# Half-precision filters with both orders prepared together, and spaced sums of the first layer's gate and up weights with the context's pass in half precision

## The chip, the cores and the metric

The kernel runs on one core of one Trainium2 chip. The metric is the device time of one execution, in microseconds (us). The core has TensorE (PE, with its weight loads as PEld), VectorE (DVE), ScalarE (ACT), GpSimd (POOL) and SyncE (SP); each takes its instructions in order, and SP, ACT and POOL also issue transfers (DMA), each on a queue of its own.

## What is computed

Two layers of a backbone over 1024 latent tokens and 256 context tokens, with 1024 channels. The first layer mixes half of its channels with a Fourier transform and half with two orders of a long convolution (Hyena); its filters are made by a small network and normalised. The second layer is a neighbourhood attention. Each layer ends with a gated feed-forward part. Cut to what the change touches:

```
h = sin(freq * (z @ w1 + b1)); h = sin(freq * (h @ w2 + b2))
h = (h @ w3).reshape(L, 2, HY_ORDER, HY_CH)
h = h * exp(-t01 * deltas)
h = h / sum(abs(h), axis=(0, 1))
v = x1 * long_conv(v, filt[:, 0], skip[0])       # order 0
v = x2 * long_conv(v, filt[:, 1], skip[1])       # order 1
u = modulate(rms_norm(x, g), shift, scale)       # shift, scale from silu(c) @ ada_w + ada_b
y = (silu(u @ w_gate) * (u @ w_up)) @ w_down     # latent and, in layer 0, context tokens
```

All inputs are float32.

## The kernel before, in words

Precision is kept by splitting an operand into a high and a low part and adding three products (high x high, high x low, low x high). Many stages do this in float16 with a scale per weight ("half precision" below, `half_split`, L1218 and L1219: ACT writes the high part, DVE the low part); others use the 4-byte format fp32r (`split`, L287 and L289). A float16 split of weights needs a scale, taken from a bound on the weights: `abs_sums` (L1251) lets ACT add up the absolute values of a tile, and `scale_cols` turns the sums into a scale.

The program is written as generators that yield between pieces of work; the caller decides by its `next` calls how the pieces interleave. That order, the buffers of each pool and a planner that orders the instructions of each engine by modelled durations set the order of the work. `issue_after` (and `follow`) asks the planner to issue something only after a given instruction. The pools that matter: "s4" (20 tiles of 128x1024 f32), "s2" (34 of 128x512 f32), the weight tags "ws", "wh" and "wl" (two tiles each), and PSUM with eight banks, six called "ps" and two "pq".

The stages up to the Winograd products of the first layer:

- `filter_mlp` (L566) makes the hidden features for 512 latent and 128 context positions. `filter_raw` (L612) multiplies them with w3 and the decay window: for each order it adds and subtracts two blocks of w3 (L626), splits them, and runs 32 matmuls of 512 columns for the latent tokens, which DVE evicts (L646).
- `filter_spectrum` (L684) turns the raw filters of an order into their spectrum: 4 families x 4 blocks x 4 frequency blocks x 3 matmuls. For each block DVE forms an operand (L706 to L713), `split` makes two fp32r parts, and `cmat` (L321) loads a float16 matrix into a "ws" tile and lets ACT convert it to fp32r in a "wh" or "wl" tile (L335). ACT evicts the results (L750). `filter_sum` (L650) interleaves the normalising sum: absolute values on ACT, a maximum (L660) and an addition (L662) on DVE.
- `ada_first` (L408) multiplies the conditioning with the first 2048 columns of the adaLN weights, which POOL's queue loads into "wh" and "wl" tiles (`mat`), and turns the result (L431 to L441). `norms` (L2140) squares the rows of the tokens (L2149), spreads the norms by small matmuls, and normalises the tokens block by block (L555 to L558). In `run` (from L2196) the adaLN product comes before the spectrum of order 0, during the filters of order 0; the filters of order 1 are woven into the spectrum of order 0.
- `in_proj` (L779) runs 16 column blocks of the input projection; the steps of the context's filters and spectra (`filt`) and of four adaLN groups (`ada`) are its fill.
- `out_proj` (L1178) runs two groups of eight column blocks; its fill is `qkv_sums` (L1253), which loads 44 weight tiles over POOL's queue and sums them on ACT: four for layer 0's first gate and up tiles, 32 for the second layer's projections, eight for layer 1. `first_scales` makes scales of them. `after1` (in `run`) normalises the context with fp32r parts.
- `ffn` for layer 0 first runs the context pass: 22 blocks x gate and up x 24 matmuls of 256 columns, weights split into fp32r by `weights`; each block's result goes through a SiLU (L1529) and a product (L1530). Then come the latent tokens by Winograd products in half precision (`wino_weights`, `wino_steps`, L1449). Where a weight tile has no scale yet, `wino_weights` takes its sums itself, on ACT, before the split.

## Time and profile before

| | |
|---|---|
| timed runs | median 2919.48 us of 3 (2914.33 to 2921.39) |
| profiled execution | 2919.95 us, span 2918.2 us |
| mean granted TensorE clock | 0.977 |
| PE busy | 2766.6 us (95% of the span) |
| DVE, ACT, POOL busy | 2094.0, 1647.7, 642.6 us |
| DMA moved | 615.98 MB, mean 211 GB/s |

Lines of the profile name the source line of an instruction (L283 is every matmul of the helper `mm`), the engine, the operation, the tile written and the tiles read, shapes and counts, then busy time, mean duration in ns, and the idle time before with what ended it. A row of stretches gives, for a stretch in us from the span's start, the busy time and the count on PE, PEld, DVE, ACT and POOL, then the granted TensorE clock as a share of full speed, the DMA engines' busy share and GB/s. A row of waits gives who waited for whom, the total us, the number of times and the longest.

### The profile page before, as it was taken

Reading aid. Unit: us, or ns where it says so; the run is one execution under the profiler, and the core shown is the slowest. Engines: PE = TensorE matmul, PEld = TensorE weight load, DVE = VectorE, ACT = ScalarE, POOL = GpSimd, SP = SyncE. Lnnn points to the kernel's source line nnn. Section 1 sums busy time; section 2 is a strip of 40 time slices with the busy share of each in tenths; the row PEclk is TensorE's granted clock in tenths of the full one; section 3 lists DMA queues with packets and bytes.
Section 4 is the critical chain, followed back from the end, with each engine's and each line's share of the span. In section 5 each row is a group of like instructions: output and inputs, shape, how many; then the busy total and the mean of one; then the engine's idle time right before and its main releaser. Section 6 shows DMA issues by size and latency. Waiting matters only on the chain. (4 is left out here: it accounts for less than half of the span.)

```text
span 2918.2 us, 46050 instructions
## 1 busy us (share of the span) xinstructions
PE 2766.6 (95%) x16163; PEld 1714.2 (59%) x16163; DVE 2094.0 (72%) x3833; ACT 1647.7 (56%) x2899; POOL 642.6 (22%) x1057
## 2 busy tenths in 40 slices
PE   6989999999989999999999999999999999999998
PEld 3766557888879644444555844676665444444554
DVE  4778867585467798877886767776676778775765
ACT  4674324454675667654555555676664477654553
POOL 1012013354220121213120012444443022112000
PEclk8989999999999999999999999999999999999999
DMA  6574434358785555566994798777775666424753
GB/s 254 187 265 161 161 122 151 111 168 286 285 344 182 207 205 197 201 213 240 327 333 161 273 337 294 179 188 172 185 198 188 236 226 231 153 93 184 242 191 113
DMA packets 325156, 615.98 MB, mean 211 GB/s; under 512 B 90934, under 2 KB 130552, under 8 KB 324922
## 3 DMA queue, kind: packets, MB, share of 16 engines
q1 hardware_dynamic: 252378, 384.38, 39.9%
q0 software_dynamic: 70240, 224.45, 21.6%
q10 hardware_dynamic: 2304, 4.20, 0.4%
q8 instruction: 127, 2.08, 0.3%
q14 instruction: 107, 0.88, 0.1%
HBM read 455.33 MB, written 135.53 MB: 202 GB/s over the span
## 5 line engine op out<-in xcount | busy, mean ns | idle before, releaser
L1449 PE MATMUL ps<-s,s 128*128 128x512 f16 x2592 | 582.2, 382 | 14.4 <-ACT tk L1454 6.8
L1449 PEld LDWEIGHTS <-s 128*128 128x128 f16 x2640 | 259.0, 98 | 332.6 <-issue 27.8
L283 PE MATMUL ps<-s,wh 128*128 128x256 f32 (+3 forms) x1752 | 398.2, 331 | 11.1 <-ACT wh L287 5.4
L1218 ACT ACTIVATE s<-s,c 128x512 f16<-128x512 f32 (+1 forms) x324 | 233.5, 754 | 141.9 <-DMA s<-d 79.9
L1219 DVE SCALAR_TENSOR_TENSOR s<-s,c,s 128x512 f16<-128x512 f32 (+1 forms) x324 | 247.4, 794 | 84.5 <-ACT s L1218 84.1
L1666 PE MATMUL ps<-s 128*128 128x512 f16 (+2 forms) x1308 | 303.4, 378 | 2.0 <-DVE s L1219 2.0
L283 PE MATMUL pq<-s,wh 128*128 128x512 f16 (+1 forms) x1000 | 280.3, 354 | 9.8 <-DMA wh<-d 5.4
L283 PE MATMUL ps<-s,wl 128*128 128x256 f32 (+3 forms) x876 | 261.6, 331 | 1.3 <-DVE wl L289 1.2
L283 PEld LDWEIGHTS <-wh 128*128 128x128 f16 x1664 | 160.9, 99 | 170.2 <-issue 20.9
L1666 PEld LDWEIGHTS <-s 128*128 128x128 f16 x1536 | 148.5, 98 | 178.9 <-issue 6.5
L274 POOL DMA_DIRECT2D d<-s x201 | 109.0, 543 | 640.5 <-DVE s L1510 178.6
L283 PE MATMUL ps<-s,s 128*128 128x65 f16 (+5 forms) x2666 | 222.3, 236 | 27.5 <-DMA s<-s 11.4
L335 ACT CAST mat<-cs 128x1024 fp32r<-128x1024 f16 (+2 forms) x120 | 111.6, 935 | 140.6 <-PE ps L283 57.3
L283 PEld LDWEIGHTS ps<-s,wh 128*128 128x128 f32 x1088 | 177.5, 192 | 18.1 <-ACT wh L287 5.7
L283 PE MATMUL ps<-s,mat 128*128 128x512 f32 x696 | 184.7, 413 | 3.3 <-DVE s L289 2.9
L1449 PE MATMUL ps<-s,wh 128*128 128x512 f16 x616 | 184.9, 379 | 1.8 <-DVE g L1463 1.4
L283 PE MATMUL pq<-s,wl 128*128 128x512 f16 (+1 forms) x500 | 174.5, 354 | 0.5 <-DMA wl<-d 0.5
L283 PEld LDWEIGHTS <-s 128*128 128x128 f16 x2400 | 114.5, 98 | 82.9 <-DMA s<-s 11.5
L283 PEld LDWEIGHTS ps<-s,mat 128*128 128x128 f32 x696 | 136.5, 199 | 37.9 <-DVE s L289 3.8
L1251 ACT ACTIVATE t<-s 128x1024 bf16<-128x1024 f32 (+1 forms) x164 | 141.9, 867 | 12.2 <-DVE c L470 8.4
L283 PEld LDWEIGHTS ps<-s,s 128*128 128x128 f32 (+1 forms) x746 | 113.6, 192 | 32.1 <-ACT s L287 7.0
L283 PEld LDWEIGHTS <-wl 128*128 128x128 f16 x832 | 82.3, 99 | 77.4 <-issue 4.5
(431 smaller groups left out, 5477.3 us busy)
## 6 DMA issues: line engine op xcount, KB each, us to landing
s<-d SPq DMA_DIRECT2D x294, 256.0 KB, 4.0
d<-s POOLq DMA_DIRECT2D x157, 256.0 KB, 3.2
s<-in_down SPq DMA_DIRECT2D x154, 256.0 KB, 5.4
s<-in_ada_w POOLq DMA_DIRECT2D x48, 512.0 KB, 4.8
g<-in_bias POOLq DMA_DIRECT2D x128, 192.0 KB, 3.6
s<-in_gate SPq DMA_DIRECT2D x46, 512.0 KB, 3.7
s<-in_up SPq DMA_DIRECT2D x46, 512.0 KB, 4.0
d<-g POOLq DMA_DIRECT2D x87, 256.0 KB, 2.9
```

Source lines behind the costliest of these rows:

```text
L274: self.last_ldr = self.nc.gpsimd.dma_start(out, in_).ins
L283: self.nc.tensor.matmul(o, l, r, start=st, stop=sp)
L335: self.nc.scalar.copy(m, st)
L1218: nc.scalar.activation(hi, src, AF.Copy, scale=scale)
L1219: nc.vector.scalar_tensor_tensor(lo, src, scale, hi, op0=MUL, op1=SUB)
L1251: self.nc.scalar.activation(junk[:, :t.shape[1]], t, AF.Abs, scale=2.0 ** -15, accum_out=st[:, k:k + 1])
L1449: nc.tensor.matmul(ps, x[:, sl], y, start=first and j == 0 and x is wh and y is xh, stop=j == 3 and x is wl, skip_group_check=True)
L1666: m = nc.tensor.matmul(acc[j][:, c0:c1], x[:, sl], y[:, xs], start=first and k == 0, stop=last and k == 2, skip_group_check=True)
```

## The change

1. Filters in half precision: the hidden features, w3 and the spectrum's operands become float16 parts; the spectrum's matrices are loaded as float16 and used directly (`mat16`), without conversion.
2. `filter_w3` (new) loads w3 for both orders, bounds it (ACT and PE), scales and splits it once, and stores the parts in DRAM, from where the context's filters load them.
3. The adaLN product uses "s4" tiles and runs in the first eight steps of the spectrum of order 0; the rows' squares are spaced over the filters of order 0.
4. POOL takes the additions of `filter_sum` and, for the latent spectrum of order 1, the operands of even blocks.
5. `gate_sums` (new) loads 32 of layer 0's 44 gate and up tiles over ACT's queue into "ws" tiles during the input projection and sums them there; `qkv_sums` takes the other twelve and the 40 it keeps: 52. `first_scales` makes all 22 scales of layer 0, so that `wino_weights` takes no sums there.
6. The context pass uses half precision: `weights3`, `norm_half`, and the scales undone at the SiLU and the product.

```diff
-PAD_C, PAD_T, SHIFT = 176, 160, 16
+PAD_C, PAD_T, SHIFT = 128, 160, 16
...
+    def mat16(self, w):
+        self.m16 = (getattr(self, "m16", 0) + 1) % 3
+        return self.pw.tile([P, w], F16, tag=("ws", "wh", "wl")[self.m16], name=self.nm("m16"))
...
+    def weights3(self, src, scale):
+        self.p3 = (getattr(self, "p3", 0) + 1) % 3
+        tags = ("ws", "ws") if self.p3 == 0 else ("wh", "wl")
+        st = self.S4()
+        hi, lo = (self.pw.tile([P, 1024], F16, tag=g, name=self.nm(n)) for g, n in zip(tags, ("wh", "wl")))
+        self.ld(st, src)
+        self.half_split(st, scale, hi, lo)
+        return hi, lo
...
-            ws = [self.mat(1024, F32) for _ in range(2)]
+            ws = [self.S4() for _ in range(2)]
...
+        self.w3d = {(o, eo): self.DR([P, 1024], F16) for o in (0, 1) for eo in (0, 1)}
+
+    def split16(self, src):
+
+        t = self.S2(F16, 1024)
+        self.nc.scalar.copy(t[:, :512], src)
+        self.nc.vector.tensor_tensor(t[:, 512:], src, t[:, :512], SUB)
+        return t[:, :512], t[:, 512:]
+
+    def filter_w3(self):
...
+        for o in (0, 1):
+            ab = self.T(BF16, 1024)
+            ps = sums[o] = self.PS()
+            for j in (0, 1):
+                nc.scalar.activation(ab[:, j * 512:j * 512 + 512], st[(o, j)], AF.Abs)
+            for j in (0, 1):
+                self.mm(ps, self.ones.bitcast(BF16)[:, 1::2], ab[:, j * 512:j * 512 + 512], j == 0, j == 1)
+        yield
+        big = self.C(4)
+        for o in (0, 1):
+            nc.vector.tensor_reduce(big[:, 2 + o:3 + o], sums[o], axis=AX, op=MAX)
+        nc.vector.tensor_scalar(big[:, 2:4], big[:, 2:4], 1e-30, 2.0 ** -14, op0=MAX, op1=MUL)
+        nc.vector.reciprocal(big[:, 0:2], big[:, 2:4])
+        yield
+        for o in (0, 1):
             for eo, op in ((0, ADD), (1, SUB)):
                 t = self.T()
...
+                nc.vector.tensor_tensor(t, st[(o, 0)], st[(o, 1)], op)
+                x = self.S2(F16, 1024)
+                self.half_split(t, big[:, o:o + 1], x[:, :512], x[:, 512:])
+                self.ldr(self.w3d[(o, eo)], x)
+                self.w3[(o, eo)] = (x[:, :512], x[:, 512:])
+            yield
...
                 if b:
-                    nc.vector.tensor_tensor(acc, acc, t, ADD)
+                    nc.gpsimd.tensor_tensor(acc, acc, t, ADD)
...
-                        (nc.vector if sq == "l" else nc.gpsimd).tensor_tensor(t, f, r, ADD if i in (0, 3) else SUB)
-                    xh, xl = self.S2(F32R), self.S2(F32R)
-                    self.split(t, xh, xl)
-                    yield xh, xl, self.cmat(2 * nb * P, a["ff_" + sq][i, b])
+                        eng = nc.vector if sq == "l" and (o == 0 or b % 2) else nc.gpsimd
+                        eng.tensor_tensor(t, f, r, ADD if i in (0, 3) else SUB)
+                    xh, xl = self.split16(t)
+                    mt = self.mat16(2 * nb * P) if sq == "l" else self.S2(F16, 256)
+                    self.ld(mt, a["ff_" + sq][i, b])
+                    yield xh, xl, mt
...
+    def gate_sums(self):
+
+        nc, a = self.nc, self.a
+        n = 32
+        self.fs = self.C(4 * (NFB // 2))
+        tiles = {}
+
+        def load(j):
+            if j < n:
+                t = tiles[j] = self.pw.tile([P, 1024], F32, tag="ws", name=self.nm("ws"))
+                self.lda(t, a[("gate", "up")[j // 2 % 2]][0, j // 4 * 2 + j % 2])
+
+        load(0)
+        load(1)
+        yield
+        for j in range(n):
+            t = tiles.pop(j)
+            nc.scalar.activation(t, t, AF.Abs, scale=2.0 ** -15, accum_out=self.fs[:, j:j + 1])
+            load(j + 2)
+            if j % 2:
+                yield
...
-                gh, gl = self.weights(a["gate"][l, fb], wide=wide)
-                uh, ul = self.weights(a["up"][l, fb], wide=wide)
+                (gs, gi), (us, ui) = (self.wsc[(l, fb // 2, m)] for m in (0, 1))
+                gh, gl = self.weights3(a["gate"][l, fb], gs)
+                uh, ul = self.weights3(a["up"][l, fb], us)
...
-                nc.scalar.activation(t[:, :256], ga[:, :256], AF.Silu)
-                nc.vector.tensor_tensor(t[:, :256], ua[:, :256], t[:, :256], MUL)
+                nc.scalar.activation(t[:, :256], ga[:, :256], AF.Silu, scale=gi)
+                nc.vector.scalar_tensor_tensor(t[:, :256], ua[:, :256], ui, t[:, :256], op0=MUL, op1=MUL)
...
-            with self.follow(self.last_hi):
-                for i, t in rows:
-                    nc.scalar.activation(t, t, AF.Square, accum_out=sq[:, i:i + 1])
+            for i, t in rows:
+                nc.scalar.activation(t, t, AF.Square, accum_out=sq[:, i:i + 1])
+                yield
...
-        for i, _ in enumerate(fr):
-            next(ada1, None)
-            if i in (0, 4):
-                next(ng)
-        drain(ada1)
-        self.u0col, self.usi = self.operand_scale(0, 0, (0, 1))
+            next(wg)
+        for i, _ in enumerate(self.filter_raw("l", raws["l"], (0,))):
+            if i == 1:
+                drain(wg)
+            next(ng)
         fr = self.filter_raw("l", raws["l"], (1,))
         for i, _ in enumerate(self.filter_spectrum("l", 0, raws["l"][0])):
+            if i < 8:
+                next(ada1)
+            elif i == 8:
+                drain(ada1)
+                self.u0col, self.usi = self.operand_scale(0, 0, (0, 1))
             if i >= 2:
                 next(fr, None)
-            if i >= 11:
+            if i < 4 or i >= 11:
                 next(ng)
...
-        self.in_proj(u, ((filt, 1), (ada, 2)))
+        gsum = self.gate_sums()
+        next(gsum)
+        self.in_proj(u, ((filt, 1), (ada, 2), (gsum, 1)))
```

103 lines of the change are left out of this document (61 added, 42 removed).

## The prediction

> **What bounds the kernel now.** I read the page first, then the table of stretches, which splits the span by stage, then the list of waits inside each stretch and the timeline where a row was unclear. The profiled execution took 2919.95 us: a span of 2918.2 us and 1.75 us around it. The median of the three timed runs is 2919.48 us, so the sum can be made against the profiled execution as it stands.
>
> ```profile
> span 2918.2 us, 46050 instructions
> PE 2766.6 (95%) x16163; PEld 1714.2 (59%) x16163; DVE 2094.0 (72%) x3833; ACT 1647.7 (56%) x2899; POOL 642.6 (22%) x1057
> ```
>
> PE is the bound as a whole, so only two things can pay: cheaper matmuls, and the stretches where PE is not full. The stretches that the change touches (busy time of PE, PEld, DVE, ACT, POOL, then granted clock, DMA share, GB/s):
>
> ```profile
> 27.00:44.00 17.00, 13.64 (x50) 6.06 (x50) 10.62 (x20) 15.93 (x34) 2.63 (x5) 0.80 0.93 360
> 44.00:69.00 25.00, 19.70 (x70) 10.79 (x68) 4.19 (x22) 8.48 (x13) 1.97 (x4) 0.65 0.40 127
> 69.00:126.00 57.00, 51.97 (x216) 40.42 (x216) 41.02 (x62) 36.33 (x52) 0.00 (x0) 0.94 0.56 185
> 126.00:198.00 72.00, 66.39 (x271) 51.83 (x270) 59.93 (x101) 54.75 (x82) 1.28 (x2) 0.91 0.58 197
> ...
> 206.00:450.00 244.00, 236.62 (x1300) 134.81 (x1299) 189.15 (x392) 88.08 (x158) 41.96 (x48) 0.97 0.44 158
> ...
> 851.00:982.00 131.00, 126.25 (x1063) 124.56 (x1064) 92.87 (x116) 75.64 (x109) 11.91 (x22) 0.97 0.64 233
> 982.00:1450.00 468.00, 457.96 (x2120) 209.71 (x2119) 391.30 (x697) 289.89 (x526) 96.07 (x178) 0.99 0.63 227
> ```
>
> In order: the latent filters of order 0; the wait for the first adaLN product; the spectrum of order 0 with the filters of order 1; the spectrum of order 1; the input projection; the context's gate and up pass; the first layer's Winograd products. The weak stretches are the second to the fourth: 154 us. The input projection and the Winograd products are PE bound.
>
> **The change part by part.** Rates first: matmuls of 512 columns in f32 and of a set of 256, 512 and 512 columns in f16; f32 ones of 256 columns; casts of the spectrum's matrices; adaLN product.
>
> ```profile
> 94.75 0.39 PE L283 MATMUL pq<-s,s 128*128 128x512 f32 x1
> ...
> 94.98 3.84 PE L283 MATMUL ps<-s,mat 128*128 128x512 f32 x16
> ...
> 428.32 0.49 PE L283 MATMUL pq<-s,wl 128*128 128x256 f16 x2
> ...
> 428.86 0.49 PE L283 MATMUL pq<-s,wh 128*128 128x256 f16 x2
> ...
> 929.98 0.28 PE L283 MATMUL ps<-s,wl 128*128 128x256 f32 x1
> ...
> 930.32 0.28 PE L283 MATMUL ps<-s,wl 128*128 128x256 f32 x1
> ...
> L335 ACT CAST mat<-cs x32: 1031/1050/1077, 46.9 to 186.8; 128x1024 fp32r<-128x1024 f16 x32
> ...
> 32.38 1.90 PE L423 MATMUL ps<-mat,c 128*2 128x512 f32 x16
> ...
> PE ps L423 <- DMA mat<-in_ada_k: 4.5, 2, 2.9
> ...
> 56.21 6.96 PE L283 MATMUL ps<-c,g 2*128 2x2 f32 x32 [0.77 <-ACT g L431]
> ```
>
> The first rows: one alone takes 0.39 us, sixteen take 3.84, so (3.84 - 0.39) / 15 = 0.230 us for each further matmul of 512 columns. The f16 set repeats every 0.54 us for 1280 columns, so 0.2165 us for 512 and 0.108 us for 256. Three f32 ones of 256 columns lie 0.34 us apart, 0.1133 each. Half precision therefore gives PE only 6%; the rest must come from waits.
>
> 1. *The wait from 44 to 69.3 us.* The latent filters of order 0 end at 44 us; the spectrum's matmuls start at 69, behind the adaLN product in PE's order. It waits for its weights, which share two tiles each of "wh" and "wl". The change moves it into the first eight steps of the spectrum and into S4 tiles: 25 us go. What it does on PE comes back there: four times sixteen instructions (4 x 1.90 = 7.6 us), and from the first of the small turns at 56.2 to 69 us the turns and the row scalings behind them (12.8 us): 20.4 us. Net -4.6, taken -4, because the order-1 weights are now prepared beside the filters of order 0: two DVE adds and two splits of about as much (below), 4 x 0.68 = 2.7 us, in a stretch where DVE is busy 10.6 of 17.
> ```profile
> PE ps L283 <- DVE s L662: 2.6, 1, 2.6
> PE pq L283 <- ACT s L287: 2.0, 1, 2.0
> ```
>
> 2. *Spectrum of order 0 and filters of order 1, 57 us.* 242 matmuls save 0.0135 us each, 3.3 us. PE's two waits in it (rows above) are 4.6 us, and the clock of 0.94 costs 3.4. Against this: the adaLN product holds one of eight PSUM banks for eight steps, and three DVE adds go to POOL. Taken -6, between -11 and 0.
> 3. *Spectrum of order 1, 72 us.* PE's own work is 210 x 0.2165 = 45.5 us and 2 us of sums. ACT loses 16 casts of 1.05 us: 54.75 - 16.85 = 37.9. DVE loses three adds of 1.21 and five of 0.68 (rows below): 59.9 - 7.0 = 52.9 us. So DVE is late next. What POOL does to it:
>
> ```profile
> 212.17 2.29 DVE L470 CUSTOM_DVE_ANT_0 s<-s,s 128x1024 f32<-128x1024 f32 x1
> ...
> 218.41 1.21 DVE L470 CUSTOM_DVE_ANT_0 s<-s,s 128x1024 f32<-128x1024 f32 x1
> ...
> L626 POOL TENSOR_TENSOR t<-s,s x4: 1266/1760/2246, 208.7 to 213.3; 128x512 f32<-128x512 f32 x4
> ...
> L660 DVE TENSOR_TENSOR s<-s,s 128x1024 f32<-128x1024 f32 x8 | 9.6, 1213 | 0.0
> ...
> L713 DVE TENSOR_TENSOR t<-s 128x512 f32<-128x512 f32 x14 | 9.5, 681 | 0.0
> ```
>
> POOL's add of 512 columns takes 1.27 us at best, of 1024 then some 2.55 (estimate, twice that). In this stretch it gets 3 x 2.55 + 5 x 1.27 = 14 us. While POOL added at 212 us, a DVE operation of 1.21 us took 2.29. [...] 53 + 5 = 58 us, -14 (between -20 and -5).
>
> [...]
>
> 4. *The adaLN loads.* 16 loads of 512 KB now run beside the spectrum, at 185 GB/s so far; +3 us taken, between 0 and 21 (third rival). Parts 1 to 4: -4 - 6 - 14 + 3 = **-21 us**.
> 5. *Input projection.* 32 absolute sums and their loads join ACT; the context filters lose 4 splits, 4 adds on POOL and 8 casts.
>
> ```profile
> L271 ACTq DMA_DIRECT2D d<-s x16: 326/326/1475, 1451.8 to 1606.3; - x16
> ...
> L1251 ACT ACTIVATE t<-s 128x1024 bf16<-128x1024 f32 x38 | 39.7, 1047 | 0.6 <-DMA s<-in_gate 0.6
> L1251 ACT ACTIVATION_READ_ACCUMULATOR t<-s 128x1 f32 x38 | 7.2, 190 | 0.0
> ...
> s<-in_gate SPq DMA_DIRECT2D x46, 512.0 KB, 3.7
> ...
> s<-in_w_in SPq DMA_DIRECT2D x16, 512.0 KB, 6.1
> ```
>
> A sum costs ACT 1.05 + 0.19 and its load 0.33 to issue: 32 x 1.57 = 50 us on 88 of 244. PE's 237 hide that while a load has landed before its sum: each is issued a step (244 / 16 = 15 us) ahead and lands in 4 to 6 us. Queued behind a late one on ACT would be the projection's evictions and the next weights' split. The context filters' some 50 matmuls save 0.7 us. Taken +0.3 in all, between -5 and +10; beyond that is the first rival.
>
> 6. *Output projection.* 52 sums instead of 44: ACT +8 x 1.24 = 9.9 us, 4.2 MB more.
>
> ```profile
> 840.00:850.00 10.00, 6.90 (x34) 5.41 (x32) 3.07 (x5) 7.65 (x16) 3.78 (x7) 0.99 1.03 420
> ...
> 851.46 0.79 PE L283 MATMUL ps<-s,wh 128*128 128x256 f32 x2 [2.33 <-ACT wh L287]
> ```
>
> At its end the DMA is full at 420 GB/s (10 us for 4.2 MB), and PE waits for a split that stands behind sums on ACT. The projection itself has no wait, so most of it is hidden: +3, between 0 and +10.
>
> 7. *Context pass.* 22 x 2 x 24 = 1056 matmuls save 0.0053 us: **-5.6**. The splits become f16 with a scale:
>
> ```profile
> L287 ACT CAST wh<-s 128x1024 fp32r<-128x1024 f32 x40 | 41.8, 1049 | 39.4 <-issue 26.4 <-PE ps L283 12.2 <-DMA s<-in_up 0.8
> ...
> L289 DVE TENSOR_TENSOR wl<-s,wh 128x1024 fp32r<-128x1024 f32 x40 | 48.9, 1225 | 26.5 <-ACT wh L287 26.5
> ...
> L1218 ACT ACTIVATE wh<-ws,c 128x1024 f16<-128x1024 f32 x21 | 24.1, 1150 | 8.4 <-PE ps L1449 5.3 <-DVE c L1317 3.0
> ...
> L1219 DVE SCALAR_TENSOR_TENSOR wl<-ws,c,wh 128x1024 f16<-128x1024 f32 x21 | 26.9, 1282 | 9.5 <-ACT wh L1218 9.5
> ```
>
> 44 x 0.06 = 2.6 us on DVE, 44 x 0.1 = 4.4 on ACT, both hidden (DVE is at 93 of 131). The last blocks now also take a "ws" tile, which the first Winograd weights want: +1, between 0 and +3.
>
> 8. *Winograd products of layer 0.* 40 sums (49.6 us of ACT's 290) go, with their 20 small matmuls.
>
> ```profile
> PE ps L1449 <- ACT g L1454: 4.2, 3, 2.9
> PE ps L1449 <- ACT tk L1454: 4.0, 2, 2.9
> ```
>
> PE waits 8.2 us for ACT here, only part of it behind a sum: -3, between -8 and 0.
>
> Sum: -21 + 0.3 + 3 - 5.6 + 1 - 3 = -25.3 us; 2919.95 - 25.3 = 2894.65, rounded **2895 us**.
>
> **The rivals.**
> *First, slower: ACT's own loads stop it in the input projection.* A step has 15 us less ACT's 5.5 + 3.1 = 8.7: some 6 us to spare. With only two "ws" tiles, loads issued just before their sums would cost two landings, 7.4 us (in_gate) to 12.2 (in_w_in); evictions and splits queue behind. Half a step's wait hides; from 6 us on, each us more costs 16. At 10 us it is 64 us: 2895 + 64 = 2959. It decides from 6 + 25/16 = 7.6 us on. For it: ACT is in order. Against: the loads are written one step ahead. Chance 0.13.
> *Second: POOL blocks DVE.* With all 14 us on DVE, the spectrum of order 1 takes 67 us, and the three adds of order 0 (7.7 us) leave nothing of part 2's gain: 2895 + 9 + 6 = 2910. For it: the row of 2.29 us. Against: POOL has a third of the time, and PE has 10 us of slack under DVE. Chance 0.17.
> *Third: the adaLN weights stay late.* The landing of those loads:
>
> ```profile
> DMA to landing us min/median/max: 3.6/6.2/9.9
> ```
>
> With one pair in flight, eight pairs take 8 x 6.2 = 50 us, while eight steps of the spectrum take about 28: PE waits some 22 instead of 3, and the 25 us are only moved: 2895 + 19 = 2914, no change to be told. S4 tiles are scarce (16 hold raw filters). Chance 0.14.
> *Fourth: everything hides.* Parts 2, 3, 4 and 8 at their best: -5 - 6 - 3 - 5 = 2876. Chance 0.08.
>
> **How the numbers follow.** Forecast 0.48, first rival 0.13, second 0.17, third 0.14, fourth 0.08. About 0.3%, 8.8 us, is what a measurement can tell from no change: faster is below 2911, slower above 2928. Forecast and fourth rival are faster, the second by half or more (0.10 of 0.17), the third in part (0.04): 0.70. Same 0.17 (the rest of the second and third); slower 0.13, the first. The range runs from 2866 (a little past the fourth rival) to 2921 (past the third) and leaves the first out.
>
> **What would show it.** The stretch between the filters of order 0 and the first spectrum matmul shrinks below 5 us; the input projection begins near 185 us instead of 206; its length stays 244; the context pass has f16 matmuls 0.108 us apart; PE's wait for the first split after the output projection grows by up to 3 us. I am wrong if the adaLN matmuls wait for their loads, if DVE's adds in the spectrum run at twice 0.68 us, or if ACT idles on "ws" loads in the input projection.

## The result and the profile after

The changed kernel takes 2942.22 us (median of 4 runs, 2938.69 to 2944.92) beside 2920.43 us of the kernel before (median of 4): about 22 us more, where 25 us less were forecast. The ratio on record is 1.0092, 95% interval 1.0072 to 1.0113; it is not the quotient of these two medians, which is 1.0075, and by it the loss would be 27 us. The page of the changed kernel shows that TensorE's work hardly fell (2763.9 us beside 2766.6), so the loss is in waits:

```profile
span 2939.4 us, 45945 instructions
...
PE 2763.9 (94%) x16147; PEld 1644.3 (56%) x16147; DVE 2088.4 (71%) x3742; ACT 1621.1 (55%) x2860; POOL 670.8 (23%) x1076
```

The input projection begins with the first high part that ACT writes of w_in. Rows of that line, of before and then of after (number of instructions, shortest, median and longest ns, first and last start):

```profile
L1218 ACT ACTIVATE wh<-s,c x16: 1136/1151/1166, 204.5 to 433.4; 128x1024 f16<-128x1024 f32 x16
```
```profile
L1279 ACT ACTIVATE wh<-s,c x60: 1132/1148/1153, 226.2 to 1004.2; 128x1024 f16<-128x1024 f32 x60
```

With the same kind of mark for the other stages (first product of the Hyena's forward part, first and last eviction of the output projection, first copy of a Winograd product out of PSUM, first weight load of the down projection), each read from the trace of one execution, the 21.2 us between the two spans fall to the stages like this:

| us | front, to the first half of w_in | input projection | Hyena | output projection | context pass | Winograd products | the rest |
|---|---|---|---|---|---|---|---|
| before | 204.5 | 270.4 | 255.4 | 115.6 | 138.0 | 397.9 | 1536.4 |
| after | 226.2 | 278.9 | 256.1 | 126.7 | 128.9 | 387.6 | 1535.0 |
| difference | +21.7 | +8.5 | +0.7 | +11.1 | -9.1 | -10.3 | -1.4 |

The table of stretches of after, in the columns of the prediction:

```profile
44.00:56.00 12.00, 5.48 (x23) 1.01 (x24) 11.96 (x21) 4.22 (x9) 0.00 (x0) 0.72 0.68 277
56.00:116.00 60.00, 59.23 (x265) 22.56 (x262) 21.63 (x39) 19.48 (x33) 3.15 (x6) 0.98 0.63 211
...
126.00:140.00 14.00, 2.38 (x7) 0.52 (x5) 7.68 (x19) 2.85 (x6) 5.29 (x3) 0.65 0.12 42
140.00:212.00 72.00, 61.17 (x254) 27.07 (x255) 54.73 (x80) 39.09 (x65) 25.31 (x11) 0.88 0.59 194
212.00:227.00 15.00, 2.10 (x10) 0.78 (x8) 0.91 (x5) 11.54 (x20) 0.00 (x0) 0.73 0.99 344
...
761.00:888.00 127.00, 116.97 (x560) 96.78 (x559) 60.10 (x96) 89.13 (x160) 34.15 (x64) 0.95 0.82 320
888.00:1016.00 128.00, 123.66 (x1080) 106.87 (x1081) 98.50 (x122) 83.49 (x112) 12.73 (x24) 0.97 0.64 229
1016.00:1404.00 388.00, 384.54 (x1776) 173.88 (x1775) 325.61 (x522) 208.22 (x386) 83.65 (x156) 1.00 0.60 214
```

The gap ahead of the first spectrum has shrunk to a wait of 6.6 us, just over the 5 that were forecast, and TensorE is full from 56 to 116 us. Two new holes follow: 126 to 140 us, with TensorE at 2.4 of 14 us, and 212 to 227, with 2.1 of 15. TensorE's two longest waits from 116 to 230 us say who ends them:

```profile
PE ps L283 <- DVE st L1385: 11.6, 1, 11.6
PE ps L283 <- POOL s L720: 8.0, 1, 8.0
```

L720 is the addition that the change moved to GpSimd; L1385 is the reduction of the first sums of w_in. GpSimd's own timeline (start, duration, then in brackets its idle time before), and the sequencer instructions of the two lines:

```profile
119.70 2.34 POOL L720 TENSOR_TENSOR s<-s,s 128x1024 f32<-128x1024 f32 x1 [37.92 <-issue]
127.56 0.38 POOL L1299 PARTITION_ALL_REDUCE c<-c  x1 [5.52 <-issue]
135.00 5.37 POOL L720 TENSOR_TENSOR s<-s,s 128x1024 f32<-128x1024 f32 x2 [7.07 <-issue]
```
```profile
L720 POOL TENSOR_TENSOR s<-s,s x6: 2337/2716/10791, 119.7 to 188.2; 128x1024 f32<-128x1024 f32 x6
...
L720 POOLq MODIFY_POOL_CONFIG  x2: 82/82/83, 127.9 to 127.9; - x2
...
L1299 POOLq MODIFY_POOL_CONFIG  x6: 6/6/37, 122.0 to 1274.0; - x6
```

The front's one all-reduce on GpSimd now stands between additions. GpSimd is idle for 5.5 us before it and 7.1 us behind it with no other engine as the cause ("issue"); changes of its configuration stand at 122.0 and at 127.9 us, where the two gaps begin. In before GpSimd ran no addition around this all-reduce: it stands alone at 64.17 us, and the 16.77 us of idle time ahead of it are put down to DVE. What GpSimd does in the two gaps was not shown; no run here isolates it.

Two more holds stand at the start. DVE's timeline, and then ACT's:

```profile
11.97 0.69 DVE L660 TENSOR_REDUCE c<-ps 128x1 f32<-128x512 f32 x1 [10.96 <-PE ps L283]
14.55 0.69 DVE L660 TENSOR_REDUCE c<-ps 128x1 f32<-128x512 f32 x1 [1.89 <-PE ps L283]
15.16 1.12 DVE L597 TENSOR_SCALAR s<-ps,c 128x512 f32<-128x512 f32 x2
```
```profile
26.92 1.28 ACT L2235 ACT_TABLE_LOAD   x1
...
28.54 1.28 ACT L607 ACT_TABLE_LOAD   x1
29.83 0.74 ACT L607 ACTIVATE s<-s 128x640 f32<-128x640 f32 x1
```

The filter net's first products end at 7.7 us, but their eviction (L597) stands on DVE behind two maxima of the new filter sums, and the second sine (29.83 us, 24.05 before) stands on ACT behind the ten row squares and two table loads.

### The profile page after: what moved, and what is told of

It reads as the page before. It is cut to its first block, busy times and chain, and to the rows that moved or that the text cites. A ratio compares the mean times of both kernels' runs of the same rounds, so it can differ in the third digit from the quotient of the medians.

```text
span 2939.4 us, 45945 instructions
## 1 busy us (share of the span) xinstructions
PE 2763.9 (94%) x16147; PEld 1644.3 (56%) x16147; DVE 2088.4 (71%) x3742; ACT 1621.1 (55%) x2860; POOL 670.8 (23%) x1076
## 5 line engine op out<-in xcount | busy, mean ns | idle before, releaser
L1534 PE MATMUL ps<-s,s 128*128 128x512 f16 x2064 | 465.6, 380 | 5.5 <-ACT g L1539 3.5
L1534 PEld LDWEIGHTS <-s 128*128 128x128 f16 x2640 | 258.4, 98 | 320.7 <-issue 9.9
L283 PE MATMUL ps<-s,wh 128*128 128x256 f16 (+3 forms) x1848 | 406.9, 329 | 13.3 <-ACT wh L287 6.2
L283 PEld LDWEIGHTS <-wh 128*128 128x128 f16 x2368 | 231.8, 99 | 186.3 <-issue 24.1
L283 PE MATMUL ps<-s,wl 128*128 128x256 f16 (+3 forms) x924 | 266.9, 328 | 1.2 <-DVE wl L1280 0.7
L1751 PEld LDWEIGHTS <-s 128*128 128x128 f16 x1536 | 148.6, 98 | 179.3 <-issue 7.4
L283 PEld LDWEIGHTS <-s 128*128 128x128 f16 (+1 forms) x2524 | 126.4, 98 | 109.5 <-issue 21.9
L1312 ACT ACTIVATE t<-s 128x1024 bf16<-128x1024 f32 (+1 forms) x153 | 129.8, 849 | 29.1 <-DMA s<-in_down 19.2
L1279 ACT ACTIVATE s<-t,c 128x512 f16<-128x512 f32 x174 | 116.3, 711 | 33.6 <-DVE t L1513 20.7
L1534 PE MATMUL pq<-s,s 128*128 128x512 f16 x576 | 133.0, 379 | 1.0 <-ACT s L1279 0.6
L1280 DVE SCALAR_TENSOR_TENSOR s<-t,c,s 128x512 f16<-128x512 f32 x174 | 125.1, 746 | 2.7 <-ACT s L1279 2.6
L1279 ACT ACTIVATE wh<-s,c 128x1024 f16<-128x1024 f32 x60 | 68.5, 1146 | 99.8 <-PE ps L283 61.9
```

The lines of the kernel that those rows point to most:

```text
L283: self.nc.tensor.matmul(o, l, r, start=st, stop=sp)
L1279: nc.scalar.activation(hi, src, AF.Copy, scale=scale)
L1280: self.last_lo = nc.vector.scalar_tensor_tensor(lo, src, scale, hi, op0=MUL, op1=SUB).ins
L1312: self.nc.scalar.activation(junk[:, :t.shape[1]], t, AF.Abs, scale=2.0 ** -15, accum_out=st[:, k:k + 1])
L1534: nc.tensor.matmul(ps, x[:, sl], y, start=first and j == 0 and x is wh and y is xh, stop=j == 3 and x is wl, skip_group_check=True)
L1751: m = nc.tensor.matmul(acc[j][:, c0:c1], x[:, sl], y[:, xs], start=first and k == 0, stop=last and k == 2, skip_group_check=True)
```

## The experiments

Ratios are to the kernel before on the same chip, with their 95% intervals. Stage lengths are of one profiled execution each, and executions of one kernel differ (e10's profiled one took 2900.6 us, its median is 2915.2), so a few us in a stage tell nothing.

**The change in two halves, and the two suspects of the front.** My first theory was that the front loses the time through GpSimd's additions and that the later stages cancel; the rival was that the sums lose it all. *e1* puts the additions of the filter sums back on DVE:

```diff
-                    nc.gpsimd.tensor_tensor(acc, acc, t, ADD)
+                    nc.vector.tensor_tensor(acc, acc, t, ADD)
```


> The changed kernel with the six additions of the normalising sum back on DVE; the operands of order 1 stay on POOL. Theory A says that POOL's additions lie around the all-reduce that gives the norm's scale, and that POOL needs 5.5 us before and 7.1 us after the all-reduce to go from one kind of work to the other: without the additions the waits of DVE for the all-reduce (3.5 us) and of PE for the sum (8.0 us) go, spectrum of order 0 ends 8 to 12 us earlier, and the time is 2928 to 2936 us. [...] Rival B expects no change, 2942 us.

*e3* starts the sums of the gate weights one step later (the `next(gsum)` ahead of `in_proj` left out):

> The changed kernel, but the first two loads of the gate and up sums are issued in the first step of the input projection and not ahead of it. In the changed kernel ACT waits 3 to 4 us each for four of these loads while the first projection weights wait for their own sums, and PE waits 11.6 us for those. If that is the cause, PE's wait falls to about 7 us as before and the time is 2935 to 2938 us. If the projection's own weights arrive late anyhow (the DMA is full there), the time stays at 2940 to 2944 us.

*e4* is before with the sums and the context pass alone, *e5* before with the filters' part (points 1 to 4 of the change) alone:

> The kernel before, with only the sums of the gate and up weights and the context pass in half precision (points 5 and 6 of the change); filters, adaLN product and norms stay as before. Theory A (the loss lies in the front, the part up to the input projection, and the rest of the change nearly cancels out): the input projection still starts at about 206 us; in the changed kernel the stretches behind the front gave +8 (input projection), +11 (output projection), -9 (context pass) and -10 us (Winograd products), so about 0 here, 2915 to 2925 us. Rival B (the sums on ACT lose it all): the input projection starts late here too, by 10 us or more, and the time is 2935 us or more.

> The kernel before, with only the filters in half precision, both orders prepared together, the adaLN product moved, the squares spaced and the additions on POOL (points 1 to 4); no new sums, the context pass in fp32r. Theory A: the input projection starts late, by 12 to 20 us, and the time is 2932 to 2942 us. Rival B: the input projection starts no later than before and the time is at or below 2920 us.

Measured: e1 1.0033 (1.0021 to 1.0045), e3 1.0091 (1.0075 to 1.0106), e4 1.0039 (1.0024 to 1.0054), e5 1.0031 (1.0016 to 1.0046). Six additions on the wrong engine cost 1.0092 - 1.0033, or 17 us; starting the gate sums a step later changes nothing. Both halves lose by themselves, so neither theory holds whole. Behind a start that is nearly unchanged (205.9 us), the stages of e4 take 279.5 (input projection), 126.1 (output projection), 131.9 (context pass) and 384.7 us (Winograd products): what the later stages lose and gain does not hang on the new front.

Where e1 gains can be read from the products of the first filter sum, first after and then e1:

```profile
140.43 3.57 PE L283 MATMUL ps<-c,s 128*128 128x1 f32 x16 [8.00 <-POOL s L720]
```
```profile
123.70 1.95 PE L283 MATMUL ps<-c,s 128*128 128x1 f32 x16 [2.63 <-DVE s L720]
```

They start 16.7 us earlier. 4.0 of these stand ahead of the additions already (the granted clock from 116 to 121 us was 0.50 in after and 1.00 in e1); most of the rest are two waits of after: DVE's 3.5 us for the all-reduce and TensorE's 8.0 for the addition. The second spectrum, from there to its last product, takes 69.2 us instead of 73.5. So Theory A of e1's expectation holds in part: the additions around the all-reduce are the larger share of the gain, and the second spectrum's 4.3 us come on top.

And in e1 the front is not faster than before either: TensorE has done its spectra near 193 us and then waits 15.1 us for the first half of w_in, at 208.7. What DVE waits for there, and the SP queue ahead of it:

```profile
207.83 0.15 DVE L1385 TENSOR_REDUCE st<-c 128x2 bf16<-128x2 f32 x1 [13.45 <-ACT tk L1312]
```
```profile
173.47 2.59 SPq L268 DMA_DIRECT2D m<-in_ff_l  x3
181.82 0.81 SPq L268 DMA_DIRECT2D d<-s  x2
...
190.87 4.48 SPq L268 DMA_DIRECT2D s<-in_w_in  x4
```

SP stands from 176 to 182 us at a store of the spectrum; w_in is queued behind it, and behind the last blocks of x.

**w_in early.** *e6* is e1 with the first two tiles of w_in loaded during the second spectrum:

```diff
+        for i, _ in enumerate(self.filter_spectrum("l", 1, raws["l"][1])):
+            next(ng, None)
+            if i in (4, 8):
+                k = i // 4 - 1
+                self.early[k] = self.S4()
+                self.ld(self.early[k], a["w_in"][k])
```


> Built on the version with the filter sums' adds on VectorE (2925.7 us, input projection's first halves at 208.7 us although its spectra end near 192), with the first two tiles of w_in loaded during the second spectrum instead of after it. Theory, the front's gain is lost to the staging of w_in behind the spectra's stores and x's loads on SP's queue: the input projection starts at 193 to 199 us and the time is 2911 to 2918 us. Rival, the transfers themselves are full there (DMA share 1.00 in 186 to 215 us), so an earlier issue only pushes x's loads back: the start stays at 204 us or later and the time at 2922 to 2928 us.

*e11* does the same to the kernel before, nothing else:

> The kernel before, with w_in's first two tiles loaded during the second spectrum and nothing else changed. Theory, the late staging is a cost that the change brings out (before waits only 5.6 us for it): the input projection starts at 197 to 201 us instead of 204.5 and the ratio is 0.997 to 0.999. Rival, the staging is a loss of its own that was there before: the start is at 188 to 193 us and the ratio 0.994 to 0.9965.

```profile
L1281 ACT ACTIVATE wh<-s,c x60: 1132/1148/1167, 191.7 to 972.3; 128x1024 f16<-128x1024 f32 x60
```
```profile
L1220 ACT ACTIVATE wh<-s,c x16: 1148/1150/1172, 193.2 to 418.9; 128x1024 f16<-128x1024 f32 x16
```

e6: 0.9986 (0.9974 to 0.9999), the input projection from 191.7 us. e11: 0.9986 (0.9971 to 1.0000), from 193.2 us. So w_in's landing ended the front, and in the kernel before too: in e4, which has before's front, TensorE has done its spectra near 192 us and waits 12.9 us for it. Of e11's expectation the rival was right on the start (193.2 us, at the edge of its 188 to 193), and the theory on the time (its ratio of 0.997 to 0.999). Until w_in is loaded early, spectra that end sooner only lengthen the wait for it.

**The two holds at the start.** *e9* (on e1) holds the row squares behind the first halves of w3, *e10* (on e6) holds the two maxima behind the first clamp:

```diff
+                with self.follow(self.last_half):
                     nc.scalar.activation(t, t, AF.Square, accum_out=sq[:, i:i + 1])
...
+            with self.follow(self.clamp):
                 nc.vector.tensor_reduce(big[:, 2 + o:3 + o], sums[o], axis=AX, op=MAX)
```


> Built on the same version, with the ten row squares held back until the first halves of the filter weights are written. Theory, the squares and the two table loads ahead of the second sin set back the front by about 6 us: the second sin is at 24 us or earlier instead of 29.8, the first raw filter is evicted at 32 to 34 us instead of 37.5, and the time falls by 3 to 6 us, to 2919 to 2923 us. Rival, the front's start has slack behind the adaLN products and the late w_in: the sin moves as said and the time stays within 2924 to 2928 us.

> The version with the sums' adds on VectorE and w_in's first tiles loaded early (2912.4 us beside 2915.1 of the kernel before, first halves of w_in at 191.7 us), with the two maxima of the filter weights' sums held back until the first layer of the filter net is clamped. Theory, VectorE's order sets the front back (the first eviction of the filter net stands at 14.6 us behind the two maxima although its products end at 7.7 us): the first sin is at 15 to 16.5 us instead of 20.0, the second at 24 to 26 instead of 29.2, the first raw filter at 32 to 34 instead of 36.6, the input projection starts at 186 to 189 us, and the time is 3 to 5 us lower, a ratio of 0.9965 to 0.9976. Rival, the front has slack further on: the sins move, the start stays at 190 to 193 us and the ratio at 0.998 to 0.9995.

e9: 1.0051 (1.0034 to 1.0068), the second sine at 28.3 us. e10: 0.9998 (0.9978 to 1.0017), the second sine at 29.1. Each hold took the other's place: with the maxima gone the clamp ends at 12.6 us but the first sine stands at 18.6 behind the squares. Neither expectation held. The maxima's hold alone gives no time; e9 could not have shown any, because it lacks the early load and w_in still starts the input projection at 208.2 us. *e12* is the filters' part alone with the additions on DVE, w_in early and the maxima late; *e18* adds the squares' hold; *e19* is e18 with the second spectrum's five operands on DVE too:

> The kernel before with the filters' part of the change alone (half-precision filters, both orders prepared together, adaLN beside the first spectrum), the sums' adds on VectorE, w_in's first tiles early and the maxima behind the clamp; no sums of the first layer and the context's pass as before. Theory, the predicted gain of the front was there and was hidden by those three: the input projection starts at 185 to 190 us, its length is 266 to 272 us, and the time is 14 to 18 us below before, a ratio of 0.994 to 0.9955. Rival, an earlier start is given back in the input projection, whose loads are then late: its length is 276 us or more and the ratio 0.996 to 0.999.

> The filters' part of the change alone with the sums' adds on VectorE, w_in early, the maxima behind the clamp and the row squares behind the filter weights' halves, both holds together (each alone left the second sin at 28 to 30 us, because the other took its place). Theory, two holds in a row set the front back by some 6 us: the second sin at 21 to 23 us, the first raw filter at 30 to 32 us instead of 37.2, the input projection from 186 to 189 us instead of 193.1 and the ratio 0.995 to 0.997 (0.998 without the squares' hold). Rival, the front is bound further on, by TensorE's own work from 56 to 116 us and VectorE's after it: the raw filters come early and the start stays at 191 to 194 us, ratio 0.9975 to 0.999.

> The same with the second spectrum's five operands on VectorE too, so that GpSimd adds nothing in the front. Theory, GpSimd's moves give VectorE no time (while GpSimd adds, VectorE's own adds take up to four times as long): the second spectrum is no longer than with them, within 2 us of the run before this one. Rival, they relieve VectorE: the spectrum is 3 to 6 us longer without them.

e12: 0.9980 (0.9966 to 0.9994), the input projection from 193.1 us, as e11, and 266.0 us long; of its theory only the length held. e18: **0.9932** (0.9919 to 0.9946), 2896.33 us; it beats both kernels. e19: 0.9939 (0.9927 to 0.9952). Of e18, the start of the input projection, ACT's sines, TensorE's wait ahead of the first spectrum, and the stretches of the front:

```profile
L1273 ACT ACTIVATE wh<-s,c x16: 1132/1149/1152, 184.8 to 408.6; 128x1024 f16<-128x1024 f32 x16
```
```profile
13.51 0.72 ACT L598 ACTIVATE s<-s 128x640 f32<-128x640 f32 x1
21.72 0.74 ACT L598 ACTIVATE s<-s 128x640 f32<-128x640 f32 x1 [7.49 <-DVE s L597]
```
```profile
43.63 0.58 PE L283 MATMUL pq<-s,c 128*2 128x512 f16 x1 [7.72 <-ACT s L624]
```
```profile
56.00:116.00 60.00, 59.23 (x252) 23.98 (x252) 23.79 (x45) 22.97 (x36) 1.05 (x2) 0.91 0.55 174
116.00:126.00 10.00, 8.09 (x40) 4.45 (x39) 9.62 (x22) 2.85 (x6) 1.29 (x1) 0.87 0.28 79
126.00:185.00 59.00, 52.80 (x231) 22.01 (x230) 54.55 (x85) 38.90 (x65) 10.43 (x7) 0.94 0.73 234
```

The squares' hold beside the maxima's gives 8 us at the start of the input projection (193.1 to 184.8), more than its theory had. The gap ahead of the first spectrum is not gone: it has moved, to 36 to 43.6 us (7.7 us; 6.6 in the changed kernel, to 50.5). The operands on GpSimd give nothing: e19 starts at 184.4 us and its interval overlaps e18's.

**Loads or passes.** The sums lengthen the input and the output projection. *e7* (on e1) and *e16* (on e10) keep the 44 loads and read 8 columns of each tile; *e8* and *e17* keep the 32 passes over one tile and leave the loads out, and the twelve of the output projection altogether:

```diff
-            nc.scalar.activation(t, t, AF.Abs, scale=2.0 ** -15, accum_out=self.fs[:, j:j + 1])
+            nc.scalar.activation(t[:, :8], t[:, :8], AF.Abs, scale=2.0 ** -8, accum_out=self.fs[:, j:j + 1])
...
+            nc.scalar.activation(tiles[1], tiles[0], AF.Abs, scale=2.0 ** -15, accum_out=self.fs[:, j:j + 1])
```


> Built on the same version; the 44 sums of the first layer's gate and up weights read 8 of each tile's 1024 columns (scaled by 128), so their loads stay and ScalarE's passes all but go (the sums are estimates and not the full ones). Theory, the loads cost: input projection about 277 us and output projection about 126 us as with full sums, time 2923 to 2928 us. Rival, the passes on ScalarE cost (44 of 1.24 us): the input projection is back at 266 to 271 us, the output projection near 116 us and the time at 2905 to 2914 us.

> Built on the same version; in the input projection one tile of the first layer's gate weights is loaded and all 32 passes read it, and the other 12 sums, in the output projection, are neither loaded nor taken (they are copies of the first 12). Theory, the loads cost: the input projection is 266 to 271 us instead of 277, the output projection 112 to 117 us instead of 126, and the time 2903 to 2913 us. Rival, the passes on ScalarE cost: the input projection stays at 274 to 278 us, only the output projection is shorter, and the time is 2912 to 2920 us.

> The change with the three repairs, 32 sums over the input projection and 12 in the output projection as written, each sum reading 8 of 1024 columns (so the sums are estimates and the passes all but gone, the loads kept). With the full passes the input projection took 275.7 us, without the sums 266.0. Theory, the loads cost: 273 to 279 us and an output projection of 125 to 129. Rival, the passes cost: 264 to 269 us.

> The same, with the passes whole over one tile of the first layer's gate weights and its 31 further loads left out, and the 12 sums of the output projection left out (copies of the first 12 stand in for them). Theory, the loads cost: an input projection of 264 to 269 us and an output projection of 112 to 117. Rival, the passes cost: 273 to 279 us.

| | ratio | input projection | output projection |
|---|---|---|---|
| e7, loads | 1.0030 (1.0014 to 1.0046) | 268.6 from 218.2 | 126.6 |
| e8, passes | 0.9987 (0.9977 to 0.9997) | 266.6 from 211.3 | 116.2 |
| e16, loads | 1.0000 (0.9983 to 1.0016) | 282.7 from 195.2 | 126.9 |
| e17, passes | 0.9920 (0.9895 to 0.9946) | 271.2 from 192.8 | 114.3 |

The times say the same in both pairs. Without the passes nothing is gained (e7 1.0030 beside 1.0033 of e1, e16 1.0000 beside 0.9998 of e10); without the loads the ratio falls to 0.9987 and 0.9920. The length of the input projection in e7 (268.6 us) would speak for the rival, but in e7 and e8 that stage starts late and at different times. From the same early start e16 is at least as long as with full sums (282.7 us, and 275.7 in e10) and e17 is shorter than e16 by 11.5 us, though both came out a few us above what the theory had. Stretches of the input projection and the landing of adaLN's weights, e16 and then e17:

```profile
215.00:260.00 45.00, 40.87 (x211) 22.11 (x211) 36.86 (x76) 16.97 (x47) 7.74 (x9) 0.92 0.88 319
260.00:300.00 40.00, 33.27 (x180) 19.78 (x179) 30.31 (x62) 21.76 (x62) 9.75 (x12) 0.91 0.82 287
```
```profile
s<-in_ada_w SPq DMA_DIRECT2D x22, 512.0 KB, 8.1
```
```profile
215.00:260.00 45.00, 39.84 (x203) 22.10 (x203) 37.47 (x77) 40.99 (x79) 9.86 (x10) 0.89 0.48 161
260.00:300.00 40.00, 37.90 (x226) 24.33 (x225) 37.64 (x86) 24.11 (x51) 13.50 (x20) 0.97 0.63 218
```
```profile
s<-in_ada_w SPq DMA_DIRECT2D x22, 512.0 KB, 4.2
```

In e17 ACT is busier (41.0 of 45 us) and TensorE still runs; in e16 the transfers are 0.8 to 0.9 busy, a 512 KB load lands in 8.1 us instead of 4.2, and TensorE has 33.3 of 40 us. Whether the full transfers delay other weights, or ACT's order stands still until a tile lands, these runs don't separate: in e16 ACT still waits for the tiles, 43.5 us in 16 pieces.

**The sums elsewhere.** *e13* takes all 44 sums in the Hyena stage, *e14* in the second half of the input projection (`half()` takes three steps of them in each of its steps 9 to 16; both on e10), *e15* is e14 with the front of before:

```diff
-        self.in_proj(u, ((filt, 1), (ada, 2), (gsum, 1)))
+        self.in_proj(u, ((filt, 1), (ada, 2), (half(), 1)))
```


> The whole change with the three repairs of the front, and all 44 sums of the first layer's gate and up weights loaded and taken during the hyena stage, whose transfers are a third to a half busy, instead of 32 in the input projection and 12 in the output projection. Theory, those loads cost where the transfers are full: the input projection is 266 to 274 us (281.6 with the sums), the output projection 110 to 117 us (126 to 128), the hyena stage 0 to 6 us longer, and the ratio 0.985 to 0.991. Rival, the sums' tiles share the staging of the hyena's matrices and stall it: the hyena stage is 12 us or more longer and the ratio 0.994 or more.

> The whole change with the three repairs of the front, and all 44 sums of the first layer in the second half of the input projection (from its ninth step, six to a step, held behind that step's split), where its transfers were 0.2 to 0.4 busy, so that the output projection has 40 sums. Theory, the sums cost only where their loads meet full transfers: the input projection is 264 to 270 us (275.7 with 32 sums spread over it), the output projection 110 to 118 us, the ratio 0.990 to 0.995. Rival, ScalarE's passes hold the evictions up: the input projection is 274 us or more and the ratio 0.997 or more.

> The same sums in the second half of the input projection and the context's pass of the change, w_in's first tiles early, but the filters, the adaLN products and the front's order as in the kernel before. Theory, the change's front gains nothing once w_in is early (both started the input projection at 193 us): within 4 us of the run before this one. Rival, the half-precision front is still worth 6 us or more when the later stages are the same: this one is slower by that.

e13: 1.0164 (1.0138 to 1.0190); the Hyena stage takes 325.6 us (e10: 253.5), so the rival held by its numbers. There ACT waits 53 us for the sums' own tiles and TensorE 36.6 us for matrices that ACT converts; whether the shared "ws" tiles or ACT's order is the cause was not separated. e14: 0.9999 (0.9982 to 1.0016), with an input projection of 294.1 us: over the 274 from which its rival decides, but the rows below show waits for loads and not passes as the cause. The output projection missed its 110 to 118 us in both, with 131.4 (e13) and 125.3 (e14) although only 40 sums are left in it. e15: 1.0022 (1.0006 to 1.0038), the Hyena from 502.9 us; it is slower than e14 by 3.9 us by the medians and by 6.7 by the ratios, on both sides of what theory and rival had, so it decides nothing on the front. ACT's waits in the second half of the input projection in e14 (380 to 488 us):

```profile
ACT ws L1350 <- DMA ws<-in_up: 25.4, 14, 3.6
ACT ws L1350 <- DMA ws<-in_gate: 16.5, 9, 5.8
```

There ACT waits 42 us for its own loads in 23 pieces, with evictions and casts behind it in its order, and TensorE stands in three waits of 8.1, 7.9 and 6.7 us, one of them for a matrix that ACT converts. This fits the mechanism of my first rival, in a place where I had put it myself.

## Why the prediction was wrong

**Parts 1 to 4, -21 us: +21.7.** This sum failed, and in it above all the terms of parts 2 and 3. Of the 21.7 us, 17.5 go with the additions (226.2 to 208.7 us in e1); the other 4.2 are the landing of w_in, which comes later in e1 than in before although e1's spectra end earlier (193 beside 198 us).
- *Part 3, "Spectrum of order 1, 72 us ... -14".* The sum books 5 us of DVE time for the additions on GpSimd, a term that no run shows. With the operands back on DVE (e19) the input projection starts as early as with them on GpSimd (184.4 beside 184.8 us), and the additions of the sums cost 17 us of the whole (e1), because they stand on the path to the sum's products (TensorE waited 8.0 us for L720) and around the all-reduce; GpSimd's idle 5.5 and 7.1 us were in no term. "PE's own work is 210 x 0.2165 = 45.5" was too small also: the rate came from a stretch of the input projection at full clock and without a wait (428 to 430 us: clock 1.00, 2.00 of 2 us busy), and the row of before (66.4 of 72 us busy) already said that this stage does not run at it. Even in e18, the 218 matmuls of the spectra between 116 and 185 us are 59.7 us busy (45.7 + 14.0, groups below), 0.274 each, at a clock of 0.87 to 0.94; DVE, which I had late next at 53 us, is 64.2 us busy there. From the products of the first sum to the last product of the spectrum, the stage takes 72.8 us in before, 73.5 in after and 67.9 in e18: 5 us less at best, where 14 were booked.
```profile
L283 PE MATMUL ps<-s,m 128*128 128x512 f16 x173 | 45.7, 406 | 3.1 <-DVE s L625 1.9 <-ACT s L624 1.2
L283 PE MATMUL pq<-s,m 128*128 128x512 f16 x45 | 14.0, 392 | 3.2 <-ACT s L803 2.4 <-DVE s L625 0.8
```
- *Parts 1 and 2, -4 and -6.* The gap shrank, but the 10 us did not come. The products of the first sum end these parts. They start at 125.4 us in before, but at 118.2, 119.5 and 119.5 in e4, e11 and e15, which have the same front; at 123.7 in e1 and 120.1 in e18. The execution that I priced had a long gap: its spectrum started at 69.4 us, theirs at 63.7 to 64.4. Part of the loss has a cause: I counted the order-1 weights as four adds and splits (2.7 us) and not the two maxima ahead of them, nor the ten squares that lost their place behind `last_hi`; both stand in front of the filter net. With the maxima held, the squares cost 8 us at the start of the input projection (e12 to e18). A moved step had been followed through its cost and not through the order of the engine that it was moved past.
- *What is late next.* I wrote that the input projection would begin near 185 us and never asked whether its weights would be there. They were not: w_in's landing ended the front at 208.7 us in e1 and at 204.5 in before (PE waited 5.6 us for it there). With it early, before starts at 193.2 us (e11) and the change's repaired filters at 184.8 (e18). By this mark the front's own gain is 8.4 us, and by TensorE's first product of the input projection (194.4 and 187.8) 6.6, where the sum had 21; the 185 us were reached with three repairs and an earlier load that the change does not contain. The ratios of e11 and e18 are further apart, by 0.0054 or 16 us, but come from two chips; no stage shows the rest.
- *Part 4, +3 and the third rival.* No wait for adaLN's weights shows from 56 to 116 us (59.2 of 60 busy): nearer to 0 than to 3.

**Part 5, input projection, +0.3: +8.5**, inside its -5 to +10. The term was mis-sized. I priced the loads by the mean of the whole stage (DMA 0.44 busy, a step of 15 us), but the planner had issued all 32 sums by 347 us:

```profile
L1349 ACT ACTIVATE ws<-ws x32: 1040/1057/1087, 200.9 to 346.8; 128x1024 f32<-128x1024 f32 x32
```

In that part of the stage the DMA is 0.88 busy (0.55 in the first 121 us of before), and adaLN's weights land in 6.9 us instead of 4.2. I had asked whether each load lands before its own sum, and not what 16.8 MB more do to the others. ACT's waits for gate and up tiles in the changed kernel are 18.5 us in nine pieces of at most 4.7, under the 7.6 us from which the first rival decides. By its number the result lies nearest to that rival (2959 us), but not by its mechanism: most of the loss stands ahead of the input projection.

**Part 6, output projection, +3: +11.1**, just past its +10. "The projection itself has no wait, so most of it is hidden" failed, and the term was mis-sized. In after TensorE waits for splits of the projection's own weights on ACT (761 to 888 us), and in e14 too (748 to 873 us); before and e15 have no such wait in this stage:

```profile
PE ps L283 <- ACT wh L287: 6.2, 3, 3.5
```
```profile
PE ps L283 <- ACT wh L287: 5.6, 2, 3.2
```

Without the passes the stage stays at 126.9 us (e16), without the loads it takes 114.3 (e17). But the number of loads alone does not decide: e14 and e15 have the same 40 sums, fewer than before, and take 125.3 and 115.8 us. What calls up these waits stays open. The stage moved 40.62 MB where before moved 33.42; the eight further tiles are 4.2 of these 7.2 MB, and the stage was also 11 us longer.

The stretches of before that answer to the last three of after above:

```profile
730.00:846.00 116.00, 113.37 (x561) 94.93 (x559) 59.79 (x96) 79.02 (x140) 30.02 (x56) 0.97 0.74 288
846.00:984.00 138.00, 129.16 (x1078) 126.29 (x1079) 96.38 (x123) 81.14 (x118) 13.34 (x25) 0.96 0.65 239
984.00:1382.00 398.00, 388.09 (x1799) 175.02 (x1799) 331.70 (x601) 249.17 (x464) 83.93 (x156) 0.99 0.58 209
```

**Part 7, context pass, -5.6 + 1: -9.1.** The products fell by 129.2 - 123.7 = 5.5 us, as worked out; the rest is waits that went (8.8 us idle before, 4.3 after). In e4, with before's front, the whole gain is 6.1 us. That the stage takes back part of what the projection before it lost is only argued: in e17, without those loads, the two together are 249.4 us, beside 253.6 in before and 255.6 in after.

**Part 8, Winograd products, -3: -10.3**, past its -8. Right in mechanism: ACT's busy time falls from 249 to 208 us and TensorE's idle time from 9.9 to 3.5. I had taken only the part of two waits that stands behind a sum and nothing for the small matmuls of the sums; 6.4 us of idle time and 3.5 of TensorE's work went. In e12, which keeps those sums, the stage is 397.9 us as before.

**The second rival** came nearest in mechanism: GpSimd was the largest cost, but as a wait for its additions more than as a block on DVE. In the changed kernel's trace both engines have operations that take longer beside the other's. An addition that takes 2.34 us at its shortest took up to 10.79 us (L720 above, from 177.35 us on) while DVE ran back to back up to 185.9 us. Beside other additions one of DVE's operations of 0.68 us took 2.83, and two took 3.81 together:

```profile
172.57 2.83 DVE L773 TENSOR_TENSOR tk<-s 128x512 f32<-128x512 f32 x1
...
189.32 3.81 DVE L634 TENSOR_TENSOR s<-t,s 128x512 f16<-128x512 f32 x2 [0.63 <-ACT s L633]
```

Here it was GpSimd that lost most, 8.45 us on one addition beside 2.15 us on DVE's one operation; what holds the one engine up while the other runs, the rows do not show.

Open: how the sums' loads cost the input projection (full transfers or ACT's order), what calls up the waits in the output projection, and what the whole change is worth with all four repairs: that combination wasn't tried. e10, with three, is at 0.9998 (0.9978 to 1.0017), e12, without the sums, at 0.9980 (0.9966 to 0.9994): whether sums and context pass together gain or lose, once spread as written, stays open.

## What to carry to other kernels

Follow a moved instruction through the order of the engine it joins: what stands behind it there, and what stands in its new place when it has gone. Before a gain at the end of a stage is booked, look at when the next stage's first weights land and behind what their load is queued; here that one load held the start of the input projection at 204 to 209 us in before, e4, e1 and e9, however early their spectra had ended. A stage's matmuls are priced at the rate of that stage, with its clock and its gaps, and added loads are priced by the transfers of the stretch in which they run, not by their own landing alone.

## What was not expected of the hardware

- In the changed kernel GpSimd stood idle 5.5 us before and 7.1 us after one all-reduce of 0.38 us between two kinds of its instructions, with a change of its configuration at the start of each gap.
- GpSimd's addition of 128x1024 took 2.34 us at its shortest in the changed kernel and up to 10.79 us beside a busy DVE.
- The median landing of a 512 KB load went from 4.2 to 8.1 us when the transfers of a stretch went from about half busy (e17) to 0.8 or 0.9 (e16); between before and the changed kernel it went from 4.2 to 6.9.
